# A two-layer attention kernel: first stage piped over features behind constant matmuls, weights laid out by partition, transposes in larger pieces

## The chip, the cores and the metric

The kernel runs on one core of a Trainium2 chip. A core has a matrix engine (PE, with a weight loader PEld), a vector engine (DVE), a scalar engine (ACT), GpSimd (POOL), a queue engine (SP) that here issues nearly all transfers, and 16 DMA engines. PE writes to PSUM banks, of which this kernel names four pairs by tag (`pj`, `mx`, `st`, `pv`). The metric is device time of one execution in microseconds (us), lower is better.

## The reference

Two layers over 1024 latent tokens and 256 context tokens of width 1024, in f32. Each layer first modulates: a vector (one for the tokens, one for the context) is multiplied by `w_mod`, which gives a shift, a scale and a gate per feature.

```python
mod_x = (silu_c @ w_mod[i] + b_mod[i])[:, None, :]
mod_c = silu_cc @ w_mod[i] + b_mod[i]
hx = rms_norm(x, norm_g[i]) * (1.0 + sc_x) + sh_x
hc = rms_norm(ctx, norm_g[i]) * (1.0 + sc_c) + sh_c
...
yx = (o * jax.nn.silu(z)) @ w_out
x = x + g_x * yx
```

Layer 0 is attention with 16 query heads over 4 key and value heads, all 1280 keys, with RMS-normed and rotated queries and keys. Layer 1 is attention in a neighbourhood of 8 by 16 positions with a bias table, plus all context keys. A last RMS norm gives the output.

## The kernel before, in words

Each f32 matrix product is made of three f16 products: both operands are split into a high and a low half, and high by high, high by low and low by high are summed in PSUM. Tokens lie in ten tiles of 128 (tiles 0 to 7 latent, 8 and 9 context), features in eight blocks `kt` of 128.

**Stage one** makes the modulated input of layer 0, transposed so that features lie on partitions, and from it keys and values of all tiles.
- `mod_cols(kt)` loads 1 MiB of `w_mod` for feature block `kt` (tiles `wm`, seven buffers), multiplies it on PE in strips of 32 columns (`pm0`, 16 instructions in the trace), copies the sums to `mrow` on DVE, brings them onto partitions with four small matmuls (`pmc0`), and DVE makes `acol` and `scol`, scale and shift of that block. `pm0` and `pmc0` each take an `mx` bank.
- `ln_pre(t)` loads a tile of x, ACT squares and sums it, DVE and POOL make the reciprocal root, DVE scales the tile (`xstage`).
- `h_kt(t0, n, kt)` transposes block `kt` of `n` tiles on PE (`pl`, a `pj` bank), ACT applies `acol` and `scol` out of PSUM into `tf` (f32), DVE casts `tf` to the high half and subtracts for the low half (`x`, for the context `xc`).
- `load_w` loads 256 KiB of the weights for k and v (`wskv`), ACT and DVE split them (`wkv`).
- `kv_mm(ps, t, kt)` is three matmuls of 512 columns; a tile needs 24. `kv_post(t)` norms, rotates and splits k, transposes it on PE (`pkt`) and copies it to `k1` and `k2`.

Tiles 0 to 3 are done block by block as weights arrive, in four banks. Tiles 4 to 9 come behind, each whole, once all blocks are there.

**Layer 0** runs over eight pairs of heads `u`: `a_proj` (query and gate, `pa`; this is where stage one ends for PE), DMA transposes of the split queries (`q16`) by groups `b` of two tiles, row maxima (`pm`), scores `st` and `qs`, exponentials, DMA transposes of probabilities (`qpp`), and products with v. `o_out` splits the output of a pair (`og`) in `oh` and `ol` and transposes each by DMA. `mod_block` makes the other modulation vectors meanwhile. Then the output product (`poa`), and **layer 1** in the same way (`pb`, `pvz`, `bsn`, `bpv`, `pob`).

The program's order on each engine is not that of the code: a `Planner` takes all instructions, gives each a cost and schedules them by list, then adds order dependences. Each engine then works its queue in that order.

Of the kernel before, what the change touches and what calls it, by code (L numbers as in the profile page):

```python
# [42 lines left out]
class Planner:  # L43
# [42 lines left out]
    def cost(self, x, rd, wr):  # L86
# [18 lines left out]
        if k == "InstDMACopy":  # L105
# [5 lines left out]
            return (430.0 if len(list(outs[0].ap)) < 3 else 550.0), m * 4 / ro * (11 + ro * 0.0432) / 16  # L111
# [42 lines left out]
    def graph(self):  # L154
        acc = {}
        self.pred = []
        self.node = []
# [11 lines left out]
        for x in self.ins:  # L169
# [11 lines left out]
            p = set()  # L181
# [29 lines left out]
            self.pred.append(p)  # L211
        self.eng = [self.ENG[x.engine.name] for x in self.node]
# [42 lines left out]
    def schedule(self, key=None, margin=0.0, scale=None):  # L255
# [4 lines left out]
        succ = [[] for _ in range(N)]  # L260
        npred = [0] * N
        for i, ps in enumerate(self.pred):
            npred[i] = len(ps)
            for p in ps:
                succ[p].append(i)
        rdy = [0.0] * N
# [143 lines left out]
        self.order, self.start, self.done, self.succ, self.came = order, start, done, succ, came  # L410
        return max(done)

    def deadlines(self, margin):
# [14 lines left out]
        for i in sorted(range(N), key=lambda i: -start[i]):  # L428
            e, d = self.eng[i], done[i] - start[i]
            for j in self.succ[i]:  # L430
                due[i] = min(due[i], due[j] - (0.0 if self.eng[j] == e == "PE" else d + self.SEM[self.eng[j]] + margin))
            for j in heirs.get(i, ()):
# [46 lines left out]
def trunk_kernel(ctx, tc, x, cx, cc, norm_g, ng_row, b_cols, sel_c, w_mod, b_mod, a_w_in, a_qg, a_kg, a_w_out,  # L479
                 b_w_in, rpb, b_w_out, fin_g, cos_t, sin_t, mask_q, out):  # L480
# [60 lines left out]
    def mod_cols(kt, pool):  # L541

        tiles = []
        for j in range(2):
            wm = pool.tile([P, 4, 2, P], F32, name=f"wm{kt}{j}", tag="wm", bufs=7)
            for r in range(2):
                a = w_mod[0, 4 * j * P:4 * j * P + P, r * D + kt * P:r * D + kt * P + 1]
                DM.dma_start(wm[:, :, r, :], bass.AP(a.tensor, a.offset, [[3 * D, P], [P * 3 * D, 4], [1, P]]))
            tiles += [wm[:, d] for d in range(4)]
        ps = ps_mx(f"pm0{kt}", shape=(P, 2, P))  # L550
        for d in range(KT):
            T.matmul(ps[32 * (d % 4):32 * (d % 4) + 32], s2[:, d, :], tiles[d], start=d < 4, stop=d >= 4)
        row = lp.tile([P, 2, P], F32, name=f"mrow{kt}", tag="mrow", bufs=1)
        V.tensor_copy(row, ps)
        pc = ps_mx(f"pmc0{kt}", shape=(P, 2, 2))
# [1060 lines left out]
```

## Time and profile before

| | |
|---|---|
| median of 3 runs | 1395.98 us (1395.3 to 1396.6) |
| the profiled execution: its time, its span | 1397.8 us, 1396.0 us |
| PE busy | 1341.6 us (96%) |
| DVE busy | 1000.0 us (72%) |
| ACT, POOL busy | 938.8 us, 648.5 us |
| DMA engines, mean busy share | 58.5% |

The span runs from the first to the last instruction. A busy PE is one with a matmul in it; a matmul at half clock is as busy as one at full clock, so durations have to be read beside the shares.

### The profile page before, as it was taken

The page shows a single profiled execution, that of the slowest core. Times are in us where ns is not written, and L with a number is a line of the kernel's source. Part 1 is how long each engine was busy: PE and PEld are TensorE (multiplying, and loading weights), DVE is VectorE, ACT ScalarE, POOL GpSimd, SP SyncE. Part 2 cuts the span into 40 slices and gives each one's busy share as a digit, 9 for nine tenths or more (in the row PEclk, how much of TensorE's full clock was granted, in tenths as well). Part 3 has the DMA queues.
Part 4 walks back from the last instruction along what each step waited for, and adds up shares of the span by engine and source line. Part 5 has one row for each costly group of instructions (what it writes and reads, how often), then busy time and mean ns, then how long its engine had stood idle before and what let it go on. Part 6 is the DMA issues. An engine that isn't in the chain of part 4 may idle for free.

```text
span 1396.0 us, 35447 instructions
## 1 busy us (share of the span) xinstructions
PE 1341.6 (96%) x13402; PEld 930.8 (67%) x13402; DVE 1000.0 (72%) x2568; ACT 938.8 (67%) x2294; POOL 648.5 (46%) x907
## 2 busy tenths in 40 slices
PE   4899999999999999999999999999999999999897
PEld 2458777777777777776654476867677686867443
DVE  2697878888789787689347756677776768687733
ACT  2463889888979777788742437677777767686811
POOL 2132778776867766687864301312122222322332
PEclk9999999999999999999999999999999999999999
DMA  8754468778676223234438735585666766597832
GB/s 258 234 125 118 98 120 134 141 151 159 139 142 136 70 62 70 57 111 109 104 97 192 188 97 114 94 157 122 128 136 116 144 112 148 97 170 149 172 109 103
DMA packets 434294, 180.97 MB, mean 130 GB/s; under 512 B 340225, under 2 KB 412865, under 8 KB 434121
## 3 DMA queue, kind: packets, MB, share of 16 engines
q1 hardware_dynamic: 433544, 178.66, 58.5%
q8 instruction: 105, 1.72, 0.5%
q14 instruction: 69, 0.56, 0.1%
q10 hardware_dynamic: 576, 0.03, 0.0%
HBM read 87.36 MB, written 12.08 MB: 71 GB/s over the span
## 4 chain that ended last, share of the span: by engine, by line
PE 56%; DVE 8%; ACT 5%; issue 3%; DMA 2%; POOL 0%; DVEq 0%; POOLq 0%; ACTq 0%; SPq 0%
PE pvz L1355 11%; PE poa L1236 7%; PE pa L917 7%; PE pb L1322 6%; PE pob L1527 5%; PE st L1143 3%; PE st L1144 2%; PE pm L947 2%; PE pv L1015 2%; PE pv L1014 2%; PE pv L1016 2%; PE bpv L1435 1%; ACT bpf L1426 1%; PE pvz L1358 1%; DVE bmx L1413 1%
## 5 line engine op out<-in xcount | busy, mean ns | idle before, releaser
L1008 POOL TENSOR_TENSOR pl<-pf,ph 128x256 f16<-128x256 f32 x400 | 273.6, 708 | 77.7 <-ACT pf L1130 61.9
L1008 POOL TENSOR_TENSOR bph<-bpf,bph 128x256 f16<-128x256 f32 (+1 forms) x128 | 99.6, 789 | 314.5 <-ACT bpf L1426 245.8
L917 PE MATMUL pa<-wa,x 128*128 128x256 f16 x1536 | 220.3, 272 | 1.0 <-DVE q16q L731 0.6
L1322 PE MATMUL pb<-hb_hi,wb 128*128 128x512 f16 (+1 forms) x640 | 191.4, 358 | 0.7 <-DVE bq L1337 0.7
L1128 ACT ACTIVATE ph<-st 128x512 f16<-128x512 f32 x240 | 143.9, 603 | 59.2 <-PE st L1144 56.2
L1355 PE MATMUL pvz<-wb,hb_hi 128*128 128x256 f16 x1024 | 174.8, 273 | 4.9 <-DVE bk L1341 3.3
L917 PEld LDWEIGHTS <-x 128*128 128x128 f16 x1536 | 140.0, 97 | 33.6 <-issue 2.5
L948 DVE TENSOR_REDUCE mxp<-pm 128x1 f32<-128x512 f32 x192 | 128.8, 684 | 25.9 <-PE pm L947 24.9
L1130 ACT ACTIVATE pf<-st 128x512 f32<-128x512 f32 x240 | 144.4, 605 | 0.3
L1322 PEld LDWEIGHTS <-wb 128*128 128x128 f16 x960 | 92.9, 98 | 75.0 <-issue 1.3
L1355 PE MATMUL pvz<-wb,hb_lo 128*128 128x256 f16 x512 | 139.7, 273 | 0.0
L1015 PE MATMUL pv<-v,ph 128*128 128x64 f16 x960 | 123.8, 195 | 0.0
L1014 PE MATMUL pv<-v,ph 128*128 128x65 f16 x960 | 123.4, 193 | 0.0
L1016 PE MATMUL pv<-v,pl 128*128 128x65 f16 x960 | 122.1, 192 | 0.6 <-POOL pl L1008 0.6
L1355 PEld LDWEIGHTS <-hb_hi 128*128 128x128 f16 x1024 | 97.1, 98 | 29.2 <-DVE bk L1341 5.1
L1008 POOL TENSOR_TENSOR qpp<-qpf,qpp 128x256 f16<-128x256 f32 (+1 forms) x158 | 93.7, 617 | 47.7 <-ACT qpf L1086 35.3
L1322 PE MATMUL pb<-hb_lo,wb 128*128 128x512 f16 (+1 forms) x320 | 114.6, 358 | 0.0
L1014 PEld LDWEIGHTS <-ph 128*128 128x128 f16 x960 | 90.9, 97 | 20.8 <-issue 0.6
L1015 PEld LDWEIGHTS <-ph 128*128 128x128 f16 x960 | 90.4, 97 | 15.2
L1016 PEld LDWEIGHTS <-pl 128*128 128x128 f16 x960 | 91.2, 99 | 10.9 <-POOL pl L1008 1.6
L1424 ACT ACTIVATE bph<-bpf,bnx 128x384 f16<-128x384 f32 (+1 forms) x128 | 68.6, 581 | 39.1 <-DVE bnx L1416 38.9
L1143 PE MATMUL st<-q,k 128*128 128x512 f16 x240 | 90.9, 379 | 0.9 <-ACT pf L1130 0.7
(261 smaller groups left out, 3678.9 us busy)
## 6 DMA issues: line engine op xcount, KB each, us to landing
wg<-in_w_mod SPq DMA_DIRECT2D x64, 256.0 KB
wsb<-in_b_w_in SPq DMA_DIRECT2D x64, 256.0 KB
wm<-in_w_mod SPq DMA_DIRECT2D x32, 256.0 KB
wsa<-in_a_w_in SPq DMA_DIRECT2D x64, 128.0 KB
xstage<-in_x SPq DMA_DIRECT2D x8, 512.0 KB
wsoa<-in_a_w_out SPq DMA_DIRECT2D x16, 256.0 KB
x<-in_x SPq DMA_DIRECT2D x8, 512.0 KB
x_d<-x SPq DMA_DIRECT2D x8, 512.0 KB
```

The costliest lines, as they stand in the source:

```text
L917: T.matmul(ps[:, :, i, :], hA(a, kt, t), wt[w][:, kt, :], start=n == 0, stop=n == 3 * KT - 1)
L948: V.tensor_reduce(mxs[i][:, t, ch:ch + 1], pm, axis=AX.X, op=ALU.max)
L1008: G.tensor_tensor(lo[:, c], p32[:, c], hi[:, c], op=ALU.subtract)
L1014: T.matmul(pv[:, t, :], hi[:, c], v[:, 0:65], start=first and t == 0, stop=False)
L1015: T.matmul(pv[:, t, 0:HD], hi[:, c], v[:, 65:129], start=False, stop=False)
L1016: T.matmul(pv[:, t, :], lo[:, c], v[:, 0:65], start=False, stop=last and t == n - 1)
L1128: S.activation(ph, st, AF.Exp)
L1130: S.activation(p32, st, AF.Exp)
L1143: T.matmul(so, k1[:, g, kc], q1[:, :, i, :], start=True, stop=False)
L1236: T.matmul(ps, lhs(a, kt), w[b][:, kt, :], start=n == 0, stop=n == 3 * KT - 1)
L1322: T.matmul(ps[:, 0:n].rearrange("p (t q) -> p t q", q=P), wt[a][:, kt, which * P:(which + 1) * P], hb[b][:, c0 // P:(c0 + n) // P, kt], st ...
L1355: T.matmul(ps[:, :, j, :], hb[a][:, t, kt], wt[w][:, kt, 256:512], start=m == 0, stop=m == 3 * KT - 1)
```

## The change

Stage one is reordered: SP's queue of loads begins with x, a run of 34 matmuls on a tile of ones stands first on PE, `mod_cols` is cut into load, `quarters` and `cols`, which share one `mx` bank; tile 4 runs three feature blocks behind tiles 0 to 3 in a bank of the `mx` pair, and tiles 5 to 7 are transposed five blocks behind. `h_kt` writes the high half from ACT, and DVE makes `tf` out of PSUM itself. `w_mod`, the weights for k and v, for q and z and for layer 1 are laid out on the host so that what a partition gets in one transfer lies in one run. `o_out` transposes high and low half in one transfer; the queries of pairs 1 to 7 are transposed by four tiles and not by two. Four small DVE instructions of layer 1 become two. The planner's cost of a plain transfer is lowered to 0.85, and a second transfer into the same tile no longer waits in its plan for the end of the first.

```diff
@@ Planner.cost
-            return (430.0 if len(list(outs[0].ap)) < 3 else 550.0), m * 4 / ro * (11 + ro * 0.0432) / 16
+            return (430.0 if len(list(outs[0].ap)) < 3 else 550.0), m * 4 / ro * (11 + ro * 0.0432) / 16 * 0.85
@@ Planner.graph
-                            p.add(r[1])
+                            (o if self.ENG[x.engine.name] == self.ENG[self.node[r[1]].engine.name] == "SP"
+                             else p).add(r[1])
@@ mod_cols
+        def load():
+            for j in range(2):
+                wm = pool.tile([P, 4, 2, P], F32, name=f"wm{kt}{j}", tag="wm", bufs=7)
+                DM.dma_start(wm, w_m0[kt, :, 4 * j:4 * j + 4])
+                tiles.extend(wm[:, d] for d in range(4))
+
+        def quarters():
+            ps = ps_mx(f"pm0{kt}")
+            pm = ps[:, 0:2 * P].rearrange("p (a b) -> p a b", a=2)
...
+        def cols():
+            ps, row = tiles
+            pc = ps[:, 2 * P:2 * P + 4].rearrange("p (a b) -> p a b", a=2)
...
@@ stage one
+    ones = lp.tile([P, 512], F16, name="ones")
+    V.memset(ones, 1.0)
+    idle = ps_mx("idle")
+    for n in range(34):
+        T.matmul(idle, ones[:, 0:P], ones, start=n == 0, stop=n == 33)
@@ h_kt
-        S.activation(tf[:, 0:n], ps, AF.Identity, scale=acol[0][:, kt, s:s + 1], bias=scol[0][:, kt, s:s + 1])
...
-        V.tensor_copy(hi[:, kt, c], tv)
-        V.tensor_tensor(lo[:, kt, c], tv, hi[:, kt, c], op=ALU.subtract)
...
+        S.activation(hi[:, kt, c], pv, AF.Identity, scale=a, bias=b)
+        V.tensor_scalar(tf, pv, a, b, op0=ALU.mult, op1=ALU.add)
+        V.tensor_tensor(lo[:, kt, c], tf, hi[:, kt, c], op=ALU.subtract)
@@ the loop
+    LAG = 3
+    for kt in range(KT + LAG):
+        if kt + 2 < KT:
+            loads(kt + 2)
...
+        if kt == 2:
+            banks[4] = ps_kv(4)
+        if kt < KT:
+            kv_mm(banks[0], 0, kt)
         if kt + 1 < KT:
-            mod_cols(kt + 1, wmp)
...
+            mod[kt + 1][2]()
+            h_kt(0, 4, kt + 1)
+        if kt < KT:
+            for t in range(1, 4):
+                kv_mm(banks[t], t, kt)
+        if kt + 2 < KT:
+            mod[kt + 2][1]()
+        if kt >= LAG:
+            h_kt(4, 1, kt - LAG)
+            kv_mm(banks[4], 4, kt - LAG)
+        if kt >= KT:
+            kv_post(banks[kt - KT], kt - KT)
+        if kt >= 5:
+            h_kt(5, 3, kt - 5)
@@ o_out
-            for dst, src in ((hi, oh), (lo, ol)):
-                DM.dma_start_transpose(dst[:, c].rearrange("p (t q) -> p t q", q=P),
-                                       src[:, 0:n].rearrange("p t f -> p (t f)"))
+            DM.dma_start_transpose(dst.rearrange("p t a q -> p (t a) q"), oo[:, 0:n].rearrange("p t a f -> p (t a f)"))
@@ b_att, end of a half
-                    for t in range(4):
-                        V.scalar_tensor_tensor(og[:, t, i * HD:(i + 1) * HD], oc[:, t], sm[:, t:t + 1],
-                                               sz[:, hf * 4 + t, i * HD:(i + 1) * HD], op0=ALU.mult, op1=ALU.mult)
+                    V.tensor_tensor(oc, oc, sm.unsqueeze(2).broadcast_to([P, 4, HD]), op=ALU.mult)
+                    V.tensor_tensor(og[:, :, i * HD:(i + 1) * HD], oc, sz[:, hf * 4:hf * 4 + 4, i * HD:(i + 1) * HD],
+                                    op=ALU.mult)
```

Counted over the whole program: PE has 34 matmuls more and no other difference in number; SP issues 656 transfers in place of 799 (plain loads of weights 232 to 152, query transposes 40 to 26 and the copies behind them 40 to 26, output transposes 70 to 35); ACT has 11 instructions more and DVE 41 fewer. On the transposed input DVE's 24 casts and 24 subtractions become 35 instructions that make `tf` out of PSUM and 35 subtractions, of each 12 over 128 columns, 8 over 256, 8 over 384 and 7 over 512.

The first place is the head of SP's queue. Before, its first eight loads (`wm` is half of the rows of one block's `w_mod` in half of its columns, 256 KiB; `xstage` is a tile of x, 512 KiB):

```order
L548 DMA wm_150<-in_w_mod 128x4x128
L548 DMA wm_153<-in_w_mod 128x4x128
L779 DMA xstage_107<-in_x 128x1024
L779 DMA xstage_108<-in_x 128x1024
L548 DMA wm_216<-in_w_mod 128x4x128
L548 DMA wm_219<-in_w_mod 128x4x128
L779 DMA xstage_109<-in_x 128x1024
L779 DMA xstage_110<-in_x 128x1024
```

Now (`wm` is 512 KiB, two make one block):

```order
L795 DMA xstage_107<-in_x 128x1024
L795 DMA xstage_108<-in_x 128x1024
L561 DMA wm_186<-in_w_m 128x1024
L561 DMA wm_188<-in_w_m 128x1024
L795 DMA xstage_109<-in_x 128x1024
L795 DMA xstage_110<-in_x 128x1024
L775 DMA wskv_199<-in_a_wkv 128x512
L561 DMA wm_230<-in_w_m 128x1024
L561 DMA wm_232<-in_w_m 128x1024
```

Block 0 of `w_mod` was complete with the tenth load, behind four tiles of x and half of block 1; now it is complete with the fourth, and the weights `wskv` of block 0 have moved from place 15 to place 7.

The second place is the head of PE's queue, with the end of the run of constant matmuls (`idle`) and block 0. Before, its first eight rows:

```order
L791 MATMUL pl00_238<-idf_66,xstage0_107 128x128
L791 MATMUL pl01_285<-idf_66,xstage0_107 128x128
L791 MATMUL pl00_238<-idf_66,xstage1_108 128x128
L791 MATMUL pl01_285<-idf_66,xstage1_108 128x128
L791 MATMUL pl00_238<-idf_66,xstage2_109 128x128
L791 MATMUL pl01_285<-idf_66,xstage2_109 128x128
L552 MATMUL pm00_156<-wm00_150,s2_84 32x256 x4
L552 MATMUL pm00_156<-wm01_153,s2_84 32x256 x4
```

Now, from the last constant matmul on:

```order
L772 MATMUL idle_149<-ones_147 128x512
L807 MATMUL pl00_257<-idf_66,xstage0_107 128x128
L807 MATMUL pl10_263<-idf_66,xstage1_108 128x128
L568 MATMUL pm00_242<-wm00_186,s2_84 32x256 x4
L568 MATMUL pm00_242<-wm01_188,s2_84 32x256 x4
L577 MATMUL pm00_242<-sel_87,mrow0_251 128x2 x2
L818 LDWEIGHTS x00_103
L818 MATMUL pkv0_238<-wkv0_141,x00_103 128x512
```

Block 0 of the modulation now stands behind two transposes and not six, and the first product for k and v of tile 0 stands before the transposes of tiles 2 and 3.

The third place is on PE in the middle of the loop, where blocks 4 and 5 of the modulation meet. `pkv4`, tile 4's sums, holds the other `mx` bank there. Now:

```order
L577 MATMUL pm04_432<-sel_87,mrow4_441 128x2 x2
L818 LDWEIGHTS x01_104
L818 MATMUL pkv0_238<-wkv0_141,x01_104 128x512
L818 LDWEIGHTS x01_104
L818 MATMUL pkv1_239<-wkv0_141,x01_104 128x512
L818 LDWEIGHTS x01_104
L818 MATMUL pkv2_240<-wkv0_141,x01_104 128x512
L818 LDWEIGHTS x01_104
L818 MATMUL pkv3_241<-wkv0_141,x01_104 128x512
L568 MATMUL pm05_485<-wm50_443,s2_84 32x256 x4
L568 MATMUL pm05_485<-wm51_445,s2_84 32x256 x4
```

Four matmuls of 512 columns stand between the last read of block 4's bank by PE and the first write of block 5, which takes the same bank once DVE has read `acol` and `scol` of block 4 out of it. Before, the two had banks of their own and 32 rows of the queue between them.

## Rows read from the trace of the kernel before

**Rows 1.** The page's head: the span, then PE's busy time, share and instructions.
```profile
span 1396.0 us, 35447 instructions
...
PE 1341.6 (96%) x13402; PEld 930.8 (67%) x13402; DVE 1000.0 (72%) x2568; ACT 938.8 (67%) x2294; POOL 648.5 (46%) x907
```

**Rows 2.** Busy us by engine in stretches; last: clock, DMA share, GB/s.
```profile
core 0: us, PE busy (x) PEld busy (x) DVE busy (x) ACT busy (x) POOL busy (x), PEclk, DMA share, GB/s
0.00:10.00 10.00, 0.00 (x0) 0.00 (x0) 0.80 (x7) 2.54 (x4) 5.54 (x11) 1.00 0.78 237
10.00:20.00 10.00, 5.13 (x27) 2.40 (x28) 3.87 (x9) 3.56 (x8) 2.21 (x4) 1.00 1.08 313
50.00:60.00 10.00, 7.93 (x44) 3.85 (x45) 5.50 (x15) 6.50 (x11) 1.96 (x3) 0.83 1.07 371
0.00:109.40 109.40, 85.48 (x508) 43.69 (x509) 69.45 (x179) 47.92 (x92) 28.02 (x36) 0.98 0.70 201
69.50:109.40 39.90, 38.02 (x213) 20.00 (x212) 38.82 (x104) 23.40 (x52) 14.20 (x13) 1.00 0.51 123
109.40:1300.00 1190.60, 1171.55 (x12412) 845.62 (x12411) 884.35 (x2277) 860.16 (x2113) 590.98 (x841) 1.00 0.59 124
200.00:450.00 250.00, 241.19 (x3094) 184.65 (x3093) 209.51 (x595) 214.59 (x497) 186.62 (x285) 1.00 0.75 144
```

**Rows 3.** Timeline of PE, start and length: products for k and v.
```profile
26.14 4.60 PE L801 MATMUL pkv<-wkv,x 128*128 128x512 f16 x11
...
35.24 2.75 PE L801 MATMUL pkv<-wkv,x 128*128 128x512 f16 x12
...
52.16 3.79 PE L801 MATMUL pkv<-wkv,x 128*128 128x512 f16 x12
```

**Rows 4.** Timeline of all engines: one feature block's modulation, first to last step.
```profile
47.64 1.07 PE L552 MATMUL pm<-wm,s 128*32 128x256 f32 x16
48.77 0.42 DVE L554 COPY mrow<-pm 128x256 f32<-128x256 f32 x1 [0.85 <-PE pm L552]
...
50.10 0.21 DVE L560 TENSOR_SCALAR scol<-pmc,bsc 128x2 f32<-128x2 f32 x1
...
50.42 0.78 ACT L793 ACTIVATE tf<-pl,scol,acol 128x512 f32<-128x512 f32 x1 [3.69 <-DVE scol L560]
```

**Rows 5.** Timeline of PE: prices at full clock (start to start).
```profile
41.53 0.50 PE L557 MATMUL pmc<-sel,mrow 128*128 128x2 f32 x4
...
82.60 3.83 PE L801 MATMUL pkv<-wkv,x 128*128 128x512 f16 x17
86.27 0.60 PE L791 MATMUL pl<-idf,xt 128*128 128x128 f32 x4
86.70 0.81 PE L801 MATMUL pkv<-wkv,x 128*128 128x512 f16 x3
```

**Rows 6.** Timeline of PE: end of the last block's products, and the first `pa`.
```profile
69.54 1.04 PE L791 MATMUL pl<-idf,xstage 128*128 128x128 f32 x8
...
109.41 0.60 PE L917 MATMUL pa<-wa,x 128*128 128x256 f16 x4
```

**Rows 7.** Timelines of ACT and SP: the fourth tile of x arrives; loads held back.
```profile
14.69 1.06 ACT L782 ACTIVATE xj<-xstage 128x1024 bf16<-128x1024 f32 x1 [0.17 <-DMA xstage<-in_x]
...
32.82 10.21 SPq L548 DMA_DIRECT2D wm<-in_w_mod  x6
```

**Rows 8.** Groups of DVE instructions by form, 0 to 133 us: busy us, mean ns.
```profile
L796 DVE CAST x<-tf 128x512 f16<-128x512 f32 x16 | 8.4, 525 | 4.7 <-ACT tf L793 4.6
...
L948 DVE TENSOR_REDUCE mxp<-pm 128x1 f32<-128x512 f32 x5 | 3.3, 684 | 0.3 <-PE pm L947 0.3
...
L796 DVE CAST xc_hi<-tf 128x256 f16<-128x256 f32 x8 | 2.3, 282 | 0.0
```

**Rows 9.** Waits of PE, 200 to 450 us: total, times, longest.
```profile
PE qpv L1094 <- DMA qpp<-qpp: 4.8, 7, 1.5
```

**Rows 10.** The query transposes on SP's queue: ns min, median, max.
```profile
L934 SPq DMA_TRANSPOSE q<-q16q x40: 1189/1214/2161, 122.9 to 657.8; - x40
```

More of the change, by code (lines that the diff above doesn't have):

```diff
@@ L156, in graph @@
         self.pred = []
+        self.after = []
         self.node = []
@@ L260, in schedule @@
         succ = [[] for _ in range(N)]
+        late = [[] for _ in range(N)]
         npred = [0] * N
         for i, ps in enumerate(self.pred):
-            npred[i] = len(ps)
+            npred[i] = len(ps) + len(self.after[i])
             for p in ps:
                 succ[p].append(i)
+            for p in self.after[i]:
+                late[p].append(i)
         rdy = [0.0] * N
@@ L409, in schedule @@
                     offer(j)
-        self.order, self.start, self.done, self.succ, self.came = order, start, done, succ, came
+            for j in late[i]:
+                rdy[j] = max(rdy[j], s)
+                npred[j] -= 1
+                if not npred[j]:
+                    offer(j)
+        self.order, self.start, self.done, self.succ, self.late, self.came = order, start, done, succ, late, came
         return max(done)
@@ L543, in mod_cols @@
         tiles = []
-        for j in range(2):
-            wm = pool.tile([P, 4, 2, P], F32, name=f"wm{kt}{j}", tag="wm", bufs=7)
-            for r in range(2):
[L547 to L552, printed above, removed]
@@ L553, in mod_cols @@
-        row = lp.tile([P, 2, P], F32, name=f"mrow{kt}", tag="mrow", bufs=1)
-        V.tensor_copy(row, ps)
-        pc = ps_mx(f"pmc0{kt}", shape=(P, 2, 2))
-        for r in range(2):
-            T.matmul(pc[:, r, :], row[:, r, :], sel, start=True, stop=True)
-        V.tensor_scalar(acol[0][:, kt, :], pc[:, 1, :], hg[:, 0, kt:kt + 1], gb[:, 0, kt:kt + 1], op0=ALU.mult,
-                        op1=ALU.add)
-        V.tensor_scalar(scol[0][:, kt, :], pc[:, 0, :], 0.5, bsc[:, 0, 0, kt:kt + 1], op0=ALU.mult, op1=ALU.add)
@@ L562, in mod_block @@
-    def mod_block(pool, l, c0):
+        def load():
[6 more added lines that the diff above has]
+            pm = ps[:, 0:2 * P].rearrange("p (a b) -> p a b", a=2)
+            for d in range(KT):
+                T.matmul(pm[32 * (d % 4):32 * (d % 4) + 32], s2[:, d, :], tiles[d], start=d < 4, stop=d >= 4)
+            row = lp.tile([P, 2, P], F32, name=f"mrow{kt}", tag="mrow", bufs=1)
+            V.tensor_copy(row, pm)
+            tiles[:] = [ps, row]
@@ new lines, in cols @@
+        def cols():
+            ps, row = tiles
+            pc = ps[:, 2 * P:2 * P + 4].rearrange("p (a b) -> p a b", a=2)
+            for r in range(2):
+                T.matmul(pc[:, r, :], row[:, r, :], sel, start=True, stop=True)
+            V.tensor_scalar(acol[0][:, kt, :], pc[:, 1, :], hg[:, 0, kt:kt + 1], gb[:, 0, kt:kt + 1], op0=ALU.mult,
+                            op1=ALU.add)
+            V.tensor_scalar(scol[0][:, kt, :], pc[:, 0, :], 0.5, bsc[:, 0, 0, kt:kt + 1], op0=ALU.mult, op1=ALU.add)
@@ L564, in mod_block @@
+        return load, quarters, cols
+    def mod_block(pool, n, l, c0):
         nm = f"{l}{c0}"
@@ L842, in trunk_kernel @@
     tc.swap_default_side()
-    for kt in range(KT):
-        h_kt(4, 4, kt)
-        if kt % 2:
-            kv_post(banks[kt // 2], kt // 2)
+    for kt in range(KT + LAG - 5, KT):
+        h_kt(5, 3, kt)
+    for t in range(3, 5):
+        kv_post(banks[t], t)
     wa = {}
@@ L861, in trunk_kernel @@
         if t < NX:
-            for kt in (2 * t - 8, 2 * t - 7):
+            for kt in range((8, 11, 14)[t - 5] - 8, (11, 14, 16)[t - 5] - 8):
                 h_kt(8, 2, kt)
```

152 lines of the change are left out of this document (77 added, 75 removed).

## The prediction

> **What bounds the kernel now.** I read the page's head first. PE is busy for 1341.6 of 1396.0 us [rows 1], so any gain has to come out of some 54 us in which PE has no matmul, or out of matmuls that run slowly. The table of stretches says where these are [rows 2]: up to 109.4 us, where the first `pa` starts [rows 6], PE is busy for 85.48 us and idle for 23.9; from there to 1300 us it is idle for 19.0 us out of 1190.6. So nearly half of the idle time lies in stage one, and behind it PE is 98.4% full: what PE gains in stage one can be carried through to the end, and little more can be had there.
>
> Within stage one the timeline shows two kinds of loss. Matmuls of 512 columns take 4.60 / 11 = 0.418 us at 26.14 us, but 2.75 / 12 = 0.229 us at 35.24, and 3.79 / 12 at 52.16 [rows 3]. These are the two levels of the clock, 1.2 and 2.4 GHz; what preceded the low level at 26 us were transposes, strips and gaps (5.13 us busy of ten [rows 2]), and the dip at 52 us shows in the granted clock, 0.83 for that stretch. The other loss is plain waiting: for loads that SP issued late because buffers were not free (10.21 us for six loads [rows 7]), and for the chain that each feature block runs through between its strips on PE and the copy on ACT, 47.64 to 51.20 us, 3.6 us in all [rows 4]. Once all blocks are there, from 69.5 to 109.4 us, PE loses only 1.9 us of 39.9, and DVE is 97% full beside it [rows 2].
>
> **What stage one has to do on PE.** At full clock, start to start [rows 5]: 17 products from 82.60 to 86.27, 0.216 us each; four transposes from 86.27 to 86.70, 0.108 each; four small matmuls 0.50 at most. A block's strips take 1.07 [rows 4]. To the first `pa`: 240 products are 51.8 us, 80 transposes 8.6, eight blocks of modulation at 1.57 are 12.6, and the transposes of k for seven tiles, 28 at no more than 0.108, are 3.0. The sum is 76.0 us. The change takes none of it away; it sets when PE can begin and how well it is fed.
>
> **The start.** From 0 to 10 us the DMA engines moved 237 GB/s, 2.37 MB, from 10 to 20 us 313 GB/s [rows 2]. The fourth tile of x was behind 3 MiB of loads, which is 12.5 us by these rates; ACT took it at 14.69 after waiting for it [rows 7], so a load is usable 2.2 us after its bytes. Now block 1 of `w_mod` is behind 4.25 MiB (two tiles of x, block 0, two tiles, 256 KiB of `wskv`, block 1): 10 + (4.46 - 2.37) / 0.313 = 16.7, usable at 18.9 us. With the chain of 3.6 us, its high half is there at 22.5 us. By then PE can have done block 0 and the modulation of block 1: two times 1.57, eight transposes 0.9, twelve products 2.6, together 6.6 us. From 22.5 us it has 76.0 - 6.6 = 69.4 us to do and, with tile 4 and the transposes of tiles 5 to 7 to fill in, something to do nearly always. Without a gap the first `pa` comes at 91.9. I add the 1.9 us that PE lost before in the full stretch: 93.8 us. That is 15.6 us sooner than 109.4.
>
> **The constant matmuls.** They can start at about 1 us, when DVE has filled `ones`. At 0.418 each 34 take 14.2 us and end at 15.2; if only as many run slowly as at 26 us, eleven [rows 3], the other 23 take 0.216 and the end is at 1 + 4.6 + 5.0 = 10.6. Block 0 of `w_mod` is behind 2 MiB, usable at 8.9 + 2.2 = 11.1 us, and the first product needs `wskv` of block 0, behind 3.25 MiB, at 15.5. So the run hides behind loads; if it stayed slow it would cost some 1 us. I take 0. Without it, the 6.6 us of first work would run at half speed.
>
> **Weights by partition.** No row shows the new form. From below, its rate is that of the stretch that moved mostly `w_mod` in 512-byte pieces, 313 GB/s; from above, 371 GB/s at 50 to 60 us, where x and tables in long rows moved [rows 2]. Block 7 is behind 13.5 MiB: usable at 50 us by the lower, at 44 by the upper. PE comes to it at 22.5 + 6 × 5.4 = 54.9 us (a block is twelve products, four transposes, 1.57, and a tile 4 share of 0.8). Loads are then not the bound at either rate; I take the lower, which is nearer in kind, and nothing for the rest of the program, where PE waits for no load of weights to speak of.
>
> **`h_kt`.** ACT's work is the same. DVE's cast from SBUF becomes an instruction that reads PSUM. Nearest rows: 0.684 us for 512 columns out of PSUM [rows 8], 0.42 for 256 [rows 4], so by a line 0.29 for 128 and 0.55 for 384. The 35 pieces are 16.1 us, the casts were 8.4 + 2.3 = 10.7 [rows 8]. Eleven more subtractions at the line's fixed part, 0.16, are 1.7. DVE gets 7.1 us more, perhaps 5 if the read is as cheap per column as a cast. It did 69.45 us up to 109.4 [rows 2], now 76.6, of which some 6 before 22.5 us; the other 70.6 at 97% end at 95.3. That is 1.5 us behind PE. Part of it (norms and copies of k of the last tiles) isn't needed for `pa`, so I leave PE's number and put the rest into a rival.
>
> **Transposes in larger pieces.** 49 transposes at 1.2 us [rows 10] leave SP's queue. What PE lost to such transfers between 200 and 450 us is 4.8 us [rows 9] of 8.8 idle [rows 2]. From one side this gives 4.8 us. From the other, queries of a pair now wait for two groups, and the high half of an output waits for the low one; behind those transfers stand `pm` and later pairs' work a whole pair ahead. I take 0. The shorter DVE form in layer 1 is off the path, 0.
>
> **The sum.** 1396.0 - 15.6 = 1380.4 us of span. The profiled execution took 1397.8, the median was 1395.98, about the span itself; so I say 1380.
>
> **Rivals.** *DVE becomes the bound.* It has no spare time from 69.5 us on, and PE's banks for later tiles come free through it. If none of the 7.1 us hides, the gain is 8.5: 1387.5. Against it, DVE is at most half busy before 60 us [rows 2], and part of its work moves there.
>
> *The clock falls again.* Between the end of the constant run and 22.5 us PE has 6.6 us of work in 12, and much of it is transposes and strips, as before 26 us, when the clock was low. Then 6.6 us become 13.2, 1.3 more than fits, and eleven products at 0.418 in place of 0.216 add 2.2: 1383.9. The Trainium skill says in "TensorE: Matmul & The Clock Gate", section "Part 4: PE-mode transpose", that a transpose doesn't count as busy for the gate as a product does. The trace agrees so far as that stretch goes; by that rule the time is this rival's, and I give it a tenth.
>
> *More is gained.* SP's shorter queue takes back the 4.8 us, or all 8.8 between 200 and 450 us: 1375.6 to 1371.6.
>
> *Slower: loads and PE wait for each other.* There are seven `wm` buffers, and a load waits for PE's strips; strips of block 5 wait for DVE's read of block 4 in the one `mx` bank, and on DVE that read stands behind the split of `wskv`, which waits for its load. Behind the strips all products are queued. Before, such a circle held SP for 10.21 us [rows 7]. It decides at the rate to which it brings loads down: at 201 GB/s, the mean up to 109.4 us [rows 2], block 7 is usable at 71 us, 16 later than PE needs it, and the gain is gone (1396.8); at 190 it is 1400. Against it, at 313 GB/s every load is 5 us ahead.
>
> *Nothing arrives at the end.* The 15.6 us would have to be lost where PE is 98.4% full: 1396.
>
> **How the numbers follow.** Forecast (1376 to 1384) 0.52; DVE bound 0.14; clock 0.10; more gained 0.13; loads and PE 0.07; nothing 0.04. A measurement of this kernel tells 0.2%, 2.8 us, from no change. Faster gets the first four less a little, 0.87; same 0.07 (the last, and the near side of the fifth), slower 0.06. The range 1371 to 1389 leaves out the last two cases and the ends of the others.
>
> **What would show it.** Right: first `pa` at 92 to 96 us; products at 0.22 us from the first; PE idle under 5 us from 23 us to `pa`; the same 19 us idle behind. Wrong: DVE idle near 0 with PE waiting for `tf` or `x` (rival one); products at 0.42 (two); `wm` loads on SP waiting for strips with DMA share low (slower); the first `pa` early but the span not.

## The result and the profile after

The changed kernel takes 1377.45 us (median of 4 runs, 1374.5 to 1380.7) against 1395.64 us for the kernel before, measured beside it (4 runs, 1395.3 to 1396.6). The ratio is 0.9869 with an interval of 0.9846 to 0.9892: 18.2 us less, where 1380 was forecast in a range of 1371 to 1389. The page's head, with PE busy for 1343.2 of 1375.4 us, answers to [rows 1]:

```profile
span 1375.4 us, 35259 instructions
...
PE 1343.2 (98%) x13436; PEld 932.3 (68%) x13436; DVE 1002.8 (73%) x2527; ACT 942.0 (68%) x2305; POOL 654.2 (48%) x907
```

The table of stretches of the changed kernel answers to [rows 2], with the same columns.

```profile
0.00:10.00 10.00, 8.53 (x31) 3.49 (x32) 2.02 (x11) 3.69 (x6) 7.00 (x13) 1.00 0.75 277
10.00:20.00 10.00, 8.02 (x60) 3.83 (x58) 6.22 (x18) 4.52 (x9) 1.50 (x3) 0.83 1.03 410
20.00:30.00 10.00, 9.92 (x79) 5.57 (x79) 6.18 (x17) 4.15 (x7) 0.55 (x1) 1.00 1.03 402
30.00:40.00 10.00, 10.00 (x77) 5.04 (x75) 7.33 (x17) 4.46 (x9) 0.07 (x1) 1.00 1.03 402
...
50.00:60.00 10.00, 7.81 (x42) 4.11 (x40) 8.94 (x22) 7.89 (x19) 6.79 (x6) 1.00 0.55 82
...
23.00:94.04 71.04, 68.08 (x428) 35.40 (x426) 62.75 (x157) 40.06 (x83) 17.44 (x19) 1.00 0.60 191
94.04:1280.00 1185.96, 1171.25 (x12415) 846.77 (x12413) 883.78 (x2233) 861.76 (x2118) 597.45 (x843) 1.00 0.58 124
```

From 20 to 50 us PE is nearly full, while the DMA engines moved 402 to 410 GB/s from 10 to 40 us. The largest hole left in stage one lies between 50 and 60 us, 2.2 us.

The timeline of PE answers to [rows 3, 5, 6]. The constant run ends at 10.9 us. Behind it block 0's strips take 1.07 us, but those of block 1, at 16.18, take 1.94: for a short while the array is slow again. The three stretches cut to size below it say when: the granted clock (third figure from the end) is 0.50 from 15.6 to 19.0 us, the lower level, 1.2 GHz, after 4.7 us in which PE was busy for 2.72.

```profile
1.47 9.40 PE L772 MATMUL idle<-ones 128*128 128x512 f16 x34 [1.47 <-DVE twos L552]
...
11.01 1.07 PE L568 MATMUL pm<-wm,s 128*32 128x256 f32 x16
...
14.29 0.39 PE L818 MATMUL pkv<-wkv,x 128*128 128x512 f16 x1 [1.05 <-ACT x L812]
...
16.18 1.94 PE L568 MATMUL pm<-wm,s 128*32 128x256 f32 x16
...
94.04 5.18 PE L965 MATMUL pa<-wa,x 128*128 128x256 f16 x46
```

```profile
10.90:15.60 4.70, 2.72 (x26) 1.35 (x25) 2.69 (x9) 3.54 (x7) 1.41 (x2) 1.00 1.04 414
15.60:19.00 3.40, 3.40 (x22) 1.11 (x20) 2.35 (x7) 0.55 (x2) 0.00 (x0) 0.50 1.03 405
19.00:23.00 4.00, 4.00 (x37) 2.43 (x36) 2.27 (x6) 1.67 (x3) 0.00 (x0) 1.00 1.02 400
```

The first `pa` starts at 94.04 us, 15.4 us earlier than in [rows 6]. That lead doesn't simply last. The summary rows of a tile (ns min, median, max; first and last start) give the first `pb`, where layer 1 begins, and the first `pob`, behind its last attention product, in the kernel before:

```profile
L1322 PE MATMUL pb<-hb_hi,wb x640: 270/379/389, 793.6 to 1265.6; 128*128 128x512 f16 x128, 128*128 128x256 f16 x32
...
L1527 PE MATMUL pob<-wob,ob x384: 376/380/381, 1286.6 to 1387.7; 128*128 128x512 f16 x192
```

and in the changed kernel:

```profile
L1367 PE MATMUL pb<-hb_hi,wb x640: 269/379/389, 779.8 to 1246.0; 128*128 128x512 f16 x128, 128*128 128x256 f16 x32
...
L1571 PE MATMUL pob<-wob,ob x384: 376/379/380, 1266.2 to 1367.1; 128*128 128x512 f16 x192
```

The first `pb` comes 13.8 us earlier and the first `pob` 20.4 us. So stage one brought 15.4 us, some 1.6 us of it was given back in layer 0, and layer 1 brought 6.6 us that the prediction doesn't have. The waits of PE in the changed kernel (total, times, longest) show the same 4.8 us for `qpp` as [rows 9], and the waits inside stage one:

```profile
PE qpv L1142 <- DMA qpp<-qpp: 4.8, 5, 1.8
...
PE pkv L818 <- ACT x L812: 1.6, 2, 1.1
...
PE pkv L818 <- DVE x L814: 1.4, 2, 1.2
```

### The profile page after: what moved, and what is told of

The parts are those of the page before. It is cut to its first block, busy times and chain, and to the rows that moved or that the text cites. A ratio compares the mean times of both kernels' runs of the same rounds, so it can differ in the third digit from the quotient of the medians.

```text
span 1375.4 us, 35259 instructions
## 1 busy us (share of the span) xinstructions
PE 1343.2 (98%) x13436; PEld 932.3 (68%) x13436; DVE 1002.8 (73%) x2527; ACT 942.0 (68%) x2305; POOL 654.2 (48%) x907
## 4 chain that ended last, share of the span: by engine, by line
PE 80%; DVE 7%; DMA 6%; ACT 5%; issue 1%; POOL 1%; SPq 0%; DVEq 0%; POOLq 0%; ACTq 0%
PE pb L1367 13%; PE pa L965 13%; PE pvz L1400 11%; PE poa L1283 7%; PE pob L1571 5%; PE st L1191 3%; PE st L1192 3%; PE bpv L1480 2%; PE pm L999 2%; PE pv L1068 2%; PE pv L1069 2%; PE pv L1067 2%; DMA qpp<-qpp 2%; PE pvz L1403 2%; PE pmg L601 1%
## 5 line engine op out<-in xcount | busy, mean ns | idle before, releaser
L965 PE MATMUL pa<-wa,x 128*128 128x256 f16 x1536 | 223.2, 272 | 0.3 <-DVE q L753 0.3
L1068 PEld LDWEIGHTS <-ph 128*128 128x128 f16 x960 | 90.6, 97 | 13.8 <-issue 0.2
```

The lines of the kernel that those rows point to most:

```text
L965: T.matmul(ps[:, :, i, :], hA(a, kt, t), wt[w][:, kt, :], start=n == 0, stop=n == 3 * KT - 1)
L1068: T.matmul(pv[:, t, 0:HD], hi[:, c], v[:, 65:129], start=False, stop=False)
```

## The experiments

**How they are compared.** Each kernel was timed beside the kernel before on one chip, whose median was 1396.97 us for e1 to e4 (with the late parts alone among them), 1398.44 for e5 to e8 and 1398.05 for e9 to e12. So ratios to the kernel before count, and the changed kernel's is 0.9869 (0.9846 to 0.9892). Two kernels whose intervals overlap aren't told apart here.

The planner makes its order anew for every kernel, so an edit can change the order of everything else. In the traces the sequence of instructions on every engine is another kernel's in three cases alone, apart from the constant matmuls: `e5` has the changed kernel's, `e6` has `e1`'s, and `e11` has that of the kernel before. `e3` has the changed kernel's until layer 1. `e2`, `e4`, `e7`, `e8`, `e9`, `e10` and `e12` differ from the kernel that they are compared with from stage one on, on one engine or more; what they measure is their edit together with another order.

**The constant run, four kernels.** The run's own work and the order that the planner makes in expectation of it are two things. `e1` takes the run out of code and plan. `e5` keeps the plan of the changed kernel and runs one matmul in place of 34; `e6` runs 34 in the plan without them. So each order is there with the run and without it.

```diff
 e1
-    idle = ps_mx("idle")
-    for n in range(34):
-        T.matmul(idle, ones[:, 0:P], ones, start=n == 0, stop=n == 33)
 e5
-    for n in range(34):
-        T.matmul(idle, ones[:, 0:P], ones, start=n == 0, stop=n == 33)
+    T.matmul(idle, ones[:, 0:P], ones, start=True, stop=True)
+            if outs[0].bass_ap.tensor.name.startswith("idle"):
+                return 34 * (512 / 2.4 + 2.5), 170.0
 e6
+            if outs[0].bass_ap.tensor.name.startswith("idle"):
+                return 0.1, 1.0
```

> The changed kernel without its 34 constant matmuls; nothing else differs. Theory: the run lifts the clock before the first block arrives, so that without it the 6.6 us of first work (two blocks of modulation, eight transposes, twelve products) go at half speed: 1.3 us more than fits before 22.5 us, and 2.2 us for eleven products at 0.418 in place of 0.216; first pa at about 97.5, total some 3.5 us above the changed kernel. Rival one: the granted clock fell to 0.83 in the stretch from 10 to 20 us with the run too, so the run buys nothing: first pa at 94, no difference. Rival two: the clock stays low until 35 us as in the kernel before; then some 12 us of products and strips at half speed cost 6 us or more, first pa at 100 or later.

> The changed kernel with one constant matmul in place of 34, while the planner still prices it as the 34: every engine's order is that of the changed kernel, only the work of 33 constant matmuls is gone. Without the run and with the planner's order changed too, the kernel took 1372.5 us, 5 us less. Theory: the run itself costs those 5 us (the granted clock falls to half for 3.4 us behind it, at 15.6 us, and again at 637 us), so without it this order gives 1372 to 1374 and no granted stretch at half speed before the end. Rival one: the order costs them; then it stays at 1377, and nothing depends on the run. Rival two, the prediction's: the run helps in this order, and without it first pa comes 3.5 us later, total 1381.

> The order of the kernel without the run, with the 34 constant matmuls ahead on PE, priced at nearly nothing by the planner. Theory (the run itself costs): 1376 to 1378, with a half-speed stretch of the granted clock between 12 and 20 us. Rival one (the order decides): 1372 to 1373. Rival two (the run helps the first products): 1369 to 1370, first pa at 90 us in place of 92.3.

| | without the run | with the 34 |
|---|---|---|
| order planned with the run | e5: first `pa` 94.49, 1381.76 us, 0.9892 (0.9873 to 0.9912) | changed kernel: 94.04, 1377.45 us, 0.9869 (0.9846 to 0.9892) |
| order planned without it | e1: 92.34, 1372.52 us, 0.9826 (0.9813 to 0.9838) | e6: 90.39, 1375.10 us, 0.9840 (0.9818 to 0.9861) |

Along a row the intervals overlap: in a fixed order the run's effect on the time can't be told from none. Down the left column they don't: the order alone is worth 9 us there. Down the right column it is 4 us by the ratios, with intervals that overlap. At the first `pa` the run gives 0.45 us in the one order and 1.95 in the other; the order gives 2.2 and 3.7. `e1` came out below all three times expected of it, and `e5` at the time of its rival two (1381), but with the first `pa` 0.45 us later and not 3.5. `e6` lies between the times of its theory and of its rivals; its first `pa` is that of rival two, and the half-speed stretch of its theory didn't come. The theory that the run itself costs the 5 us between the changed kernel and `e1` is out, since without it `e5` is no faster; what is left is the order: of its 9 us in the left column 2.2 are there at the first `pa` (94.49 against 92.34 us) and 7.9 at the first `pb` (783.9 against 776.0), so most of it comes in layer 0. Which step of the plan does it isn't settled.

What the run does to the clock is plain from `e1`'s timeline of PE, where the first strips and products go at half speed until 19 us (1.89 us for four products, 0.47 each):

```profile
10.40 1.94 PE L568 MATMUL pm<-wm,s 128*32 128x256 f32 x16
...
14.95 1.89 PE L812 MATMUL pkv<-wkv,x 128*128 128x512 f16 x4 [1.05 <-ACT x L806]
...
16.98 1.94 PE L568 MATMUL pm<-wm,s 128*32 128x256 f32 x16
...
92.34 4.66 PE L959 MATMUL pa<-wa,x 128*128 128x256 f16 x40
```

With the run, the first 4.7 us behind it go at full speed, and then the granted clock falls. In eight of the nine profiled kernels with the run it is below 1.00 somewhere between 10 and 40 us (`e6` is the exception); in the five without it (`e1`, `e4`, `e5`, `e12` and the kernel before) it is 1.00 there. Since `e5` and the changed kernel differ in nothing but 33 matmuls, and only the latter has the fall there, the run is its likely cause in that order; each has one profiled execution.

**The run in the kernel before.** Same lines added ahead of its first stage; the order on every engine stays that of the kernel before.

> The kernel before with the 34 constant matmuls ahead on PE and nothing else. Theory: the kernel before does its first work at half speed until 30 us (eleven products at 0.418, strips at 1.94 in place of 1.07), but PE waits for loads between them, so the run gives at most 1 to 2 us: 1394 to 1397, with first pa at 107 to 110. Rival one: all the half-speed work counts, 5 us less: 1391. Rival two: the run ends long before the first product, at 10.9 us against 24.7 us, so that nothing is left of it but half-speed stretches: 1396 to 1400.

1392.82 us, ratio 0.9958 (0.9942 to 0.9975), first `pa` at 105.89 us in place of 109.41: some 6 us less by the ratio, more than the theory's 1 to 2. As the order is the same, this is the run's own work, and the one pair of kernels in which it is told from none. Rival one's price is met, yet only in part for its reason. Block 0's strips stand in the timeline at 16.87 us with 1.93 us before, and here at 15.06 with 1.07; but the eleven products that [rows 3] has at 26.14 still go at half speed, only earlier:

```profile
15.06 1.07 PE L552 MATMUL pm<-wm,s 128*32 128x256 f32 x16
...
21.88 4.85 PE L807 MATMUL pkv<-wkv,x 128*128 128x512 f16 x11
...
105.89 0.60 PE L923 MATMUL pa<-wa,x 128*128 128x256 f16 x4
```

The granted clock was 0.66 from 20 to 30 us and 0.83 from 30 to 40 us. So in this kernel the run saves more than the half-speed stretches behind it cost; in the two orders above its effect isn't told from none.

**Old layouts, the rest of the change kept.** All weights go back to their old places; in stage one `w_mod` comes in 512-byte pieces again. The code keeps the order of the loads, but the planner doesn't: SP's queue begins with two loads of `w_mod`, as in the kernel before, and not with x.

```diff
-                DM.dma_start(wm, w_m0[kt, :, 4 * j:4 * j + 4])
+                for r in range(2):
+                    a = w_mod[0, 4 * j * P:4 * j * P + P, r * D + kt * P:r * D + kt * P + 1]
+                    DM.dma_start(wm[:, :, r, :], bass.AP(a.tensor, a.offset, [[3 * D, P], [P * 3 * D, 4], [1, P]]))
...
```

> The changed kernel with all weights in their old layouts (512-byte and 1-KiB pieces, the old number of transfers), order of the loads kept. Theory: a load is hidden as long as it is ahead of PE; at the 313 GB/s that the old pieces reached in the kernel before, block 7 is usable at 50 us and PE needs it at 54.9, so little is lost: first pa at 94 to 96, total 0 to 3 us above the changed kernel. Rival: the changed kernel's loads ran at 400 to 410 GB/s from 10 to 40 us, and this is what fed PE; at 237 GB/s, the rate of the first 10 us of the kernel before, block 7 is usable only at 62 us, 7 us behind PE's need, and first pa comes at 101. A second rival concerns layer 1, which got 6.8 us shorter: if the laid out weights of layer 1 are the reason, that part of the lead is lost here too, total 6 to 10 us above.

1385.3 us, ratio 0.9922 (0.9910 to 0.9935), 7.4 us above the changed kernel by the ratios; first `pa` at 105.62 us, 11.6 us later than with the new layouts. The first rival holds in kind, and the loss at the first `pa` is larger than its 101 us. The second rival's time is met, but not by its cause (below). The head of SP's queue, two stretches (as above) and the waits of SP's queue up to 60 us:

```profile
0.72 1.01 SPq L563 DMA_DIRECT2D wm<-in_w_mod  x2
1.78 0.98 SPq L809 DMA_DIRECT2D xstage<-in_x  x2
```

```profile
20.00:30.00 10.00, 8.30 (x60) 4.72 (x59) 4.04 (x12) 2.85 (x5) 0.00 (x0) 0.81 0.94 273
30.00:40.00 10.00, 10.00 (x68) 4.87 (x65) 4.60 (x10) 2.82 (x6) 0.55 (x1) 0.83 0.83 232
```

```profile
SPq L563 <- PE pm L570: 8.6, 3, 4.4
SPq L786 <- DVE acol L580: 2.8, 1, 2.8
```

At a DMA share of 0.83 to 0.94 they move 232 to 273 GB/s, where the new layouts get 402 at 1.03; the last block's strips start at 55.5 us in place of 46.4. SP waits 8.6 us for strips of PE: the circle of loads and buffers that the prediction had as its slower rival. That the rate goes with the pieces and not with the order, all fourteen traces bear out: divided by the share, the stretches from 10 to 40 us give 262 to 296 GB/s in the four kernels with the old layouts (the kernel before has 313 at 1.08 [rows 2], which is 290) and 379 to 399 in the ten with the new ones. How much of the 11.6 us is the rate's and how much the order's isn't told apart; the new layouts in the old order were not run. Most of layer 1's gain is there all the same (488.0 us from the first `pb` to the first `pob`, against 486.4 in the changed kernel and 493.0 before), so the layout of its weights isn't needed for it.

**The late parts.** `e4` is the kernel before with single output transposes, queries by four tiles and the short DVE form of layer 1; `e7` is the changed kernel without the three. `e3`, `e9` and `e10` each undo one.

```diff
 e3
-                    V.tensor_tensor(oc, oc, sm.unsqueeze(2).broadcast_to([P, 4, HD]), op=ALU.mult)
-                    V.tensor_tensor(og[:, :, i * HD:(i + 1) * HD], oc, sz[:, hf * 4:hf * 4 + 4, i * HD:(i + 1) * HD],
-                                    op=ALU.mult)
+                    for t in range(4):
+                        V.scalar_tensor_tensor(og[:, t, i * HD:(i + 1) * HD], oc[:, t], sm[:, t:t + 1], ...)
 e9
-            DM.dma_start_transpose(dst.rearrange("p t a q -> p (t a) q"), oo[:, 0:n].rearrange("p t a f -> p (t a f)"))
+            for dst, src in ((hi, oh), (lo, ol)):
+                DM.dma_start_transpose(dst[:, c].rearrange("p (t q) -> p t q", q=P), ...)
 e10
-            c = slice(0 if u else 2 * (b % 2), 2 * (b % 2) + 2)
+            c = slice(2 * (b % 2), 2 * (b % 2) + 2)
```

> The kernel before with the late parts of the change alone: outputs transposed in one transfer, queries of pairs 1 to 7 by four tiles, two DVE instructions for four in layer 1. Stage one, layouts and planner are as before. Theory: the 6.8 us by which layer 1 got shorter come from these parts (fewer DVE and SP steps between a pair's last product and the next pair's first), so this kernel is 5 to 7 us below the kernel before, and layer 1's waits of pvz on DVE are gone. Rival: layer 1 got shorter because of the layout of its weights or the planner's costs; then this kernel is within 2 us of the kernel before and those waits remain.

> The changed kernel without the late parts: outputs transposed in two transfers, queries by two tiles, four DVE instructions in layer 1; stage one, layouts and planner as changed. The late parts alone took 9.0 us off the kernel before. Theory: the parts add up, so this kernel is 8 to 9 us above the changed one, 1386, and pvz waits on DVE are back in layer 1. Rival: the late parts and the earlier stage one give partly the same (an earlier start fills the same waits), then it is at 1380 to 1383. First pa at 94 either way.

> The changed kernel with the four small DVE instructions of layer 1 in place of the two; nothing else differs. They cost 4 x 0.28 us for each half against two instructions of 256 columns. Theory: DVE's queue sits between the attention product and the next pair's products in layer 1, so that the lead of layer 1 (6.8 us) goes mostly: total 4 to 7 us above the changed kernel. Rival: the form is off the path, as the prediction had it, and the lead comes from the single transposes or the layouts: within 1 us of the changed kernel.

> The changed kernel with each output tile transposed in two transfers (35 transfers more on SP's queue), queries by four tiles and the short DVE form of layer 1 kept. All late parts undone together cost 7 to 8 us. Theory: the single transfer for the outputs is most of that, since the lead of layer 1 grows pair by pair (6.8 us over eight pairs) and layer 1 has no query transposes by DMA: 1382 to 1384, and waits of bpv on the transposes of bph are back above 3 us. Rival: the outputs' transfers are off the path and the gain is the DVE form's and the queries': within 2 us of the changed kernel.

> The changed kernel with the queries of all pairs transposed by two tiles (14 transposes and 14 copies more), all else as changed. Theory: these lie in layer 0 alone, ahead of the transposes of qpp that PE waits for (4.8 us in the changed kernel, 4.8 before), and are worth 0 to 2 us: 1377 to 1379. Rival one: they are the larger part of the late gain: 1381 to 1384. Rival two: waiting for four tiles delays pm, and by two tiles it is better: 1374 to 1375.

| | median us | ratio to before |
|---|---|---|
| e4, late parts alone on the kernel before | 1387.99 | 0.9927 (0.9916 to 0.9939) |
| e7, changed kernel without them | 1385.67 | 0.9918 (0.9895 to 0.9941) |
| e3, four DVE instructions | 1380.10 | 0.9877 (0.9865 to 0.9890) |
| e9, outputs in two transfers | 1384.57 | 0.9896 (0.9873 to 0.9919) |
| e10, queries by two tiles | 1374.08 | 0.9829 (0.9807 to 0.9851) |

By the ratios, the late parts together are worth 6.8 us (0.9918 less 0.9869, times 1396) on the new stage one and 10.2 us alone, each with a change of order in it. `e4` shows how much that can be: its first `pa` comes at 107.1 us, 2.3 us ahead of the kernel before, though no late part stands in stage one. Undone singly, the outputs' transfers cost most (3.8 us by the ratio, though the interval overlaps the changed kernel's, and though 2.7 us are lost at the first `pa` already, which is at 96.7); the DVE form, undone in the same order until layer 1, costs 1.1 us, not the 4 to 7 of its theory and not told from none; the queries' larger transposes gain nothing that can be told, and the time is that of rival two.

What holds over all the orders is the length of layer 1, from the first `pb` to the first `pob`, in the one profiled execution of each kernel. Without late parts it is 493.0 us (the kernel before), 493.9 (`e11`) and 495.8 (`e7`). In the eight kernels that have stage one of the change and all late parts of layer 1 it is 485.0 to 488.0; with one of the two undone 490.2 (`e3`) and 488.3 (`e9`). So the gain of layer 1 goes with the late parts. `e4` has both and 490.5: alone they bring 2.5 of the 6.6 us of this stage in the kernel before, while undoing them in the changed kernel costs 9.4 (`e7`). PE's busy time in layer 1 from 850 to 1000 and from 1000 to 1150 us, in the order: kernel before, changed kernel, `e7`, `e3`, `e9`:

```profile
850.00:1000.00 150.00, 148.36 (x1337) 107.25 (x1335) 110.91 (x319) 110.75 (x321) 36.63 (x51) 1.00 0.65 126
1000.00:1150.00 150.00, 147.63 (x1398) 111.52 (x1397) 106.61 (x311) 107.82 (x316) 37.74 (x53) 1.00 0.64 125
```

```profile
850.00:1000.00 150.00, 149.86 (x1399) 112.42 (x1397) 109.84 (x306) 110.54 (x321) 39.23 (x54) 1.00 0.61 123
1000.00:1150.00 150.00, 149.68 (x1402) 110.02 (x1401) 110.03 (x303) 111.50 (x325) 38.50 (x53) 1.00 0.66 132
```

```profile
850.00:1000.00 150.00, 147.76 (x1367) 108.72 (x1365) 105.53 (x313) 108.81 (x317) 37.95 (x51) 1.00 0.63 125
1000.00:1150.00 150.00, 147.41 (x1424) 112.20 (x1422) 111.40 (x320) 108.66 (x317) 38.30 (x52) 1.00 0.63 125
```

```profile
850.00:1000.00 150.00, 149.34 (x1387) 111.67 (x1385) 110.01 (x326) 108.49 (x319) 37.92 (x53) 1.00 0.63 123
1000.00:1150.00 150.00, 149.11 (x1402) 109.87 (x1400) 110.87 (x320) 111.35 (x325) 37.73 (x53) 1.00 0.64 130
```

```profile
850.00:1000.00 150.00, 149.81 (x1376) 109.96 (x1374) 106.81 (x301) 109.69 (x318) 37.29 (x51) 1.00 0.65 128
1000.00:1150.00 150.00, 149.92 (x1443) 113.99 (x1441) 108.33 (x304) 110.57 (x327) 40.47 (x58) 1.00 0.64 125
```

Out of these 300 us PE is idle for 4.0 in the kernel before and 4.8 in `e7`, with neither part; for 1.6 with single transposes alone (`e3`), 0.3 with the short DVE form alone (`e9`), and 0.5 with both (in `e4` 1.6). Either one takes most of the holes away, so undoing one of them costs little. What fills the holes is seen in PE's waits of this stretch, first in the kernel before, then in `e7`:

```profile
PE pvz L1355 <- DVE bk L1341: 2.9, 4, 0.9
PE pvz L1355 <- DVE bsz L1371: 1.0, 3, 0.3
```

```profile
PE bpv L1481 <- DMA bpht<-bph: 2.7, 4, 1.3
PE pvz L1401 <- DVE bk L1387: 2.0, 3, 1.0
```

So `pvz` waits for DVE's instructions on `bk` and `bsz`, and in `e7` `bpv` for its transposes too. `e4` and `e9` missed signs of theirs: in `e4` 1.5 us of the waits of `pvz` remain, and in `e9` `bpv` waits for 0.8 us in the whole run, not above 3.

In layer 0, from the first `pa` to the first `pb`, `e9` and `e7` with two transfers take 692.9 and 692.7 us, the changed kernel 685.8. PE waits for `qpp` for 8.8 and 6.9 us in them, for 4.8 in the changed kernel. But the kernel before has two transfers, 684.2 us and 4.8 us of that wait, and `e5`, with single ones, has 689.4 and 6.5. So two transfers went with a longer layer 0 behind the new stage one only, and that they are its cause is not shown. The row of waits of `e9`:

```profile
PE qpv L1148 <- DMA qpp<-qpp: 8.8, 8, 2.2
```

A single transfer carries both halves and takes hardly longer on the queue than one half did: by the summary rows (ns min, median, max) 1250 ns, where the high half took 1200 and the low half 1257 in the kernel before:

```profile
L1077 SPq DMA_TRANSPOSE oa<-oo x14: 1233/1250/1335, 187.5 to 644.8; - x14
```

**The old form of `h_kt`**, in the changed kernel and in `e1`.

```diff
-        S.activation(hi[:, kt, c], pv, AF.Identity, scale=a, bias=b)
-        V.tensor_scalar(tf, pv, a, b, op0=ALU.mult, op1=ALU.add)
+        S.activation(tf[:, 0:n], ps, AF.Identity, scale=acol[0][:, kt, s:s + 1], bias=scol[0][:, kt, s:s + 1])
+        V.tensor_copy(hi[:, kt, c], tv)
...
```

> The changed kernel with the old form of h_kt: ACT writes tf, DVE casts it from SBUF and subtracts; nothing else differs. DVE loses some 5 to 7 us of work up to 90 us. Theory: DVE is 97 to 99% full from 50 to 90 us in the changed kernel, and PE waits there for its x, tf and t2k (2.2 us idle from 50 to 60 us), so the old form gives first pa at 91 to 92 and 1374 to 1376. Rival one: DVE's full stretch is hidden, no difference. Rival two: the high half now waits for ACT and then DVE, so the chain of a block is 0.5 us longer or more at each of eight blocks, and first pa comes at 96 to 98, total 1380 or more.

> The changed kernel without the run and with the old form of h_kt. Each alone took the time to 1372.5 and 1374.7. Theory: both times differ from the changed kernel's only by the granted clock (0.998 against 0.995, 4 us; span times clock is 1369 us in all three), so together they give the same 1371 to 1374. Rival: DVE's relief is a gain of its own behind the order without the run, where DVE is 99 to 100% full from 50 to 90 us; then 1368 to 1370, first pa at 90 us.

`e8`: 1374.74 us, 0.9835 (0.9814 to 0.9855), first `pa` at 94.01 us, as in the changed kernel (94.04). `e12`: 1374.79 us, 0.9828 (0.9807 to 0.9849), first `pa` at 94.58, later than `e1`'s. `e8` has the time of its theory, but not the first `pa` (91 to 92); `e12` lies above both of its ranges. The form together with the order that comes with it makes no difference at the first `pa` in the one pair and costs 2.2 us in the other, and none to the time that these intervals would tell. The new form does cost DVE work: the instructions that make `tf` in the changed kernel take 5.6, 5.4, 4.8 and 4.2 us by form, 20.0 together, the casts of `e8` 11.8. Of PE's 3.0 us of idle time from 23 us to the first `pa`, 2.0 are waits for DVE's `x` and `tf` (1.4 and 0.6).

## Why the prediction was right

**The time and the first `pa`.** 1380 against 1377.45, and 93.8 against 94.04 us. PE's idle time from 23 us to the first `pa` was forecast under 5 us and is 3.0; the granted clock is 1.00 from 19 us on. The frame was right: from 10.9 to 94.04 us PE is busy for 78.2 us, 3.4 of them at half clock, which leaves 76.5 at full clock (an estimate) where 76.0 were forecast; the high half of block 1 is there at 21.7 us (22.5 forecast). Nearly all of the idle time lies between 52 and 61 us, and not behind 69.5, where the prediction took its 1.9 from.

**Weights by partition, priced at nothing: the step that failed inside stage one.** It held that loads aren't the bound at 313 GB/s or at 371. The new layouts moved 402 to 410 from 10 to 40 us, above the upper bound, and `e2` with the old ones 273 and 232 from 20 to 40, below the lower; there the first `pa` comes 11.6 us later. PE also comes to the last block's strips at 46.4 us, not at 54.9: with block 7 usable at 50 us, as the prediction has it at 313 GB/s, loads would have been the bound by 3.6 us. So the step that failed is that of the rate; its term is worth more than nothing, up to 11.6 us at the first `pa`, a change of order included. Everything but the layouts brings 3.8 of the 15.4 us (`e2`). That the sum was right all the same is because it was made from PE's work, on the ground that loads keep up, and with the new layouts they do; for a rate that it had too low, that is luck in part. In the slower rival, 71 us at 201 GB/s also leaves out the 2.2 us that the prediction adds elsewhere.

**The constant run, priced at nothing.** It ended at 10.9 us (10.6 forecast) and cost nothing. The reason given for it, that without it the first work goes at half speed, is right (`e1`); its worth by the terms of the clock rival, 3.5 us, is not: 0.45 to 1.95 us at the first `pa`, since part of the same work goes at half speed with it too. In the order of the kernel before it is 3.5 us there (`e11`). The rival of the falling clock happened, for 3.4 us, and cost less than its 3.5 us. No run tells whether transposes or gaps brought it on, so the rule on transposes that the prediction took from the Trainium skill is neither borne out nor refuted.

**`h_kt`.** The 35 instructions that make `tf` were priced at 16.1 us and take 20.0. PE waits for DVE's `x` and `tf` for 2.0 us in stage one; the rival that makes DVE the bound at 7.1 us is out, since all of PE's idle time from 23 us to the first `pa` is 3.0.

**The larger transposes and the DVE form, each priced at nothing: the step that failed behind stage one.** Together they are some 7 us by the ratios (`e7`), a change of order included. The prediction looked for the transposes' worth in layer 0's 4.8 us alone, which are still there, and took layer 1's DVE form to be off the path; but in layer 1 of the kernel before `pvz` waits on DVE for 3.9 us of 4.0 idle in 300, and either part takes most of such holes away. Layer 1 got 6.6 us shorter. The forecast that the same 19 us stay idle behind stage one was wrong with it: from 94.04 to 1280 us PE idles for 14.7.

**The sum.** It was 15.6 + 0. By the ratios, the change without the late parts gives 11.4 us (`e7`), and the late parts 6.8: 18.2. So two misses of opposite sign met, and that the total came within 3 us is luck in part. Without the late parts some of the stage's lead isn't kept: `e7` has its first `pa` 14.6 us ahead of the kernel before and its end 11.4. In its trace layer 0 takes 692.7 us in place of 684.2; it is the slowest of its runs, with half-speed stretches behind 200 us, and why layer 0 is longer isn't settled. An order alone was worth 9 us between `e5` and `e1`, more than any of these parts, and the prediction has no term for it.

**The best version seen** is the changed kernel without the constant run (`e1`), 1372.52 us, with an interval below the changed kernel's and the kernel before's. `e6`, `e8`, `e10` and `e12` aren't told from it.

## What to carry to other kernels

Where a stage is fed by loads, look at the rate for a full share of the DMA engines before pricing the order of the loads: with `w_mod` in 512-byte pieces it was 262 to 296 GB/s here, with runs of 2 and 4 KiB 379 to 399, in every order that was run. When a run of warming work is added to a kernel whose order is planned, its price in the plan can matter more than the work; run it with the plan of either, as in the four kernels above, before judging it. The same holds for every other edit: most of the kernels here got a new order with theirs. And an edit that takes small work off a second engine in a loop is priced by what waits for that engine in that loop, not by its share of the span.

## What the runs showed of the hardware

From 10 to 40 us the sixteen DMA engines moved 402 to 410 GB/s at a share of 1.03 with runs of 2 and 4 KiB for each partition, and in `e2` 327, 273 and 232 GB/s at shares of 1.14, 0.94 and 0.83 with `w_mod` in pieces of 512 bytes (x and `wskv` in rows of 4 and 2 KiB among them): 390 to 398 GB/s for a full share against 280 to 290. The Trainium skill, in "DMA: Bandwidth & Descriptors", section "Specifications", gives 512 bytes as the least transfer for line rate; the trace doesn't agree here, and the measurement decides.

The column of the granted clock doesn't show all slow work: in `e1` it reads 1.00 from 10 to 20 us, while the four products at 14.95 us take 0.47 us each.

```profile
10.00:20.00 10.00, 8.40 (x49) 3.75 (x50) 5.71 (x17) 3.91 (x8) 1.41 (x2) 1.00 1.03 409
```

What the Trainium skill says in "TensorE: Matmul & The Clock Gate", section "Part 1: The HAM clock gate (the "warmup" mystery)", that the array begins slow and activity releases it, agrees with that row.

The spread of the changed kernel's times goes with its half-speed stretches. Its four runs took 1374.5 to 1380.7 us at mean granted clocks of 0.997 to 0.992; span times clock, an estimate of the time at full clock, is 1367.8 to 1369.9 us in all four. `e1` has five runs within 1.3 us at 0.998 to 0.999, and its span times clock, 1367.9 to 1369.0, is the changed kernel's.
